# Weight differences and sums of the feed-forward beginnings made by adding transfers, on one Trainium2 core

## The chip, the core and the metric

The kernel runs on one core of a Trainium2 chip. A core has five engines with queues of their own: TensorE (PE, matrix products), VectorE (DVE), ScalarE (ACT), GpSimd (POOL) and SyncE (SP, which here only issues transfers). Transfers run on 16 DMA engines that the queues share. An engine takes its instructions in order; one that waits holds up all behind it on the same engine. The metric is the device time of one execution in microseconds.

## The reference

A two-layer encoder on `x` of 512 tokens by 1024 features, in float32. Only the feed-forward halves are touched by the change:

```python
def swiglu(x, w_gate, w_up, w_down):
    return (jax.nn.silu(x @ w_gate) * (x @ w_up)) @ w_down

for l in range(DEPTH):                                    # DEPTH = 2
    x = x + 0.5 * swiglu(rms_norm(x, ffn1_norm[l]), ffn1_w_gate[l], ffn1_w_up[l], ffn1_w_down[l])
    h = rms_norm(x, mix_norm[l]); p = h @ w_in[l]
    ...                                                   # attention and convolution groups, output projection
    x = x + 0.5 * swiglu(rms_norm(x, ffn2_norm[l]), ffn2_w_gate[l], ffn2_w_up[l], ffn2_w_down[l])
    x = rms_norm(x, post_norm[l])
```

The hidden width is 2816, that is 22 blocks of 128.

## The kernel before

**Precision.** Every float32 operand of PE is split in two numbers of a shorter format: `hi`, the rounded value, and `lo`, the rest. A product is then three matmuls (`mm3`, L145 to L147). The split of a weight of 128x1024 is a cast on ACT (`hi`, tile `wh`, L228) and a subtraction on DVE (`lo`, tile `wl`, L230), both in `split_into`. `wpool` holds four tiles `wh` and four `wl`; a split has to wait until PE has used the tile it takes over.

**Feed-forward.** `ffn_body` is called four times: layer 0 first and second, layer 1 first and second. The work is cut into six units of hidden blocks (`UNITS`), and the weights of a unit come as tiles `fr` of 512 KB, loaded by SP into nine buffers. Unit 0 is `opening()`: four weights, 96 matmuls. At its end the norm is known (`norm()`, a reciprocal root on POOL, L163), and the gate and the transposes (`gated` L356 and L357, `turn` L366) follow. A block goes through DRAM to be turned into the layout of the next product: four small transfers out (`d`, L372) and two back in (`r`, L378), in `moved`; `halved` (L384, L385) splits what came back.

Units 1 to 5 use seven products instead of eight (`product`, named b11, b21, t2, t3, t1, t4, b22; 24 matmuls each). They need sums of weights and of the inputs. The inputs' sums are made by a generator of twelve small steps, which `ops.advance(n)` moves on by n (six in the opening, three times two in unit 1); the steps are `scaled` (L269) and `signed` (L157, L158, in `split_scaled`). The weights' sums are `add`, two halves of 128x1024 each on DVE (L326). In unit 1 the sums a21 and s3 are made already by transfers that add to what is in the buffer (`fetch` with `more`, L318, issued by POOL): eight buffers `fr` and eight `raw` over the four calls. A transfer that adds can only be issued by POOL.

In the output projection eight of the weights take another way to `lo`: ACT writes the negative rounded value (L137), and an adding transfer from DRAM puts the weight on it (L138).

**Between the layers.** The last norm of layer 0 isn't applied to `x` at once. The products of layer 1's first feed-forward use the norm's factor at the gate (`NormPost.__call__`), and `norm.post()` spreads the factor over the partitions (L197 on DVE, L201 on PE, L207 on ACT) and scales the eight blocks of `x` (L973 on DVE) in unit 1. It has to be done before the first down product adds to `x`, which is in unit 2. For the other calls `post` does nothing.

**Order.** The program is written in one stream, and a scheduler of the framework lays down the order of the instructions on each engine; `between(i)` marks where the down products of the unit before are put. In the first call (`lead` is not empty) `x` is still being loaded during the opening.

Of the kernel before, what the change touches and what calls it, by code (L numbers as in the profile page):

```python
# [8 lines left out]
FR = mybir.dt.float32r  # L9
BF = mybir.dt.bfloat16  # L10
I32 = mybir.dt.int32
AF = mybir.ActivationFunctionType
ALU = mybir.AluOpType
AX = mybir.AxisListType

P = 128
# [17 lines left out]
WC = 1024  # L34
HS = S // 2
UNITS = (2, 4, 4, 4, 4, 4)
FIRST = (0, 4, 12, 20, 28, 36)
# [33 lines left out]
def encoder_kernel(ctx: ExitStack, tc: tile.TileContext, xT, consts, vecs, rgain, wgu1, wd1,  # L71
# [6 lines left out]
    wpool = ctx.enter_context(tc.tile_pool(name="w", bufs=4))  # L78
# [6 lines left out]
    def nm(s):  # L85
        uid[0] += 1
        return f"{s}{uid[0]}"
# [4 lines left out]
    def tmp(w=S, dt=FP):  # L92
        return tmps.tile([P, w], dt, tag="t", name=nm("t"))

    def bank():
        return psum.tile([P, S], FP, tag="ps", name=nm("ps"))

    def tiny(tag, w, dt=FP):
        return small.tile([P, w], dt, tag=tag, name=nm(tag))

    V, A, G, T = nc.vector, nc.scalar, nc.gpsimd, nc.tensor
# [23 lines left out]
    def vv(l, name):  # L125
        o, w = VOFF[name]
        return vec[:, l, o:o + w]
# [16 lines left out]
    def mm3(o, lh, ll, rh, rl, first, last, free=False):  # L144
        T.matmul(o, lh, rh, start=first, stop=False, skip_group_check=free)  # L145
        T.matmul(o, lh, rl, start=False, stop=False, skip_group_check=free)  # L146
        T.matmul(o, ll, rh, start=False, stop=last, skip_group_check=free)  # L147
# [68 lines left out]
    def groups(srcs, rhs, ws=None):  # L216
# [5 lines left out]
                group(o, w, rhs, ks, KD)  # L222
        return os

    def split_into(q, src, w=WC):

        hi = wpool.tile([P, WC], FR, tag="wh", name=nm("wh"))
        A.copy(hi[:, :w], src[:, :w])  # L228
        lo = wpool.tile([P, WC], FR, tag="wl", name=nm("wl"))
        V.tensor_tensor(lo[:, :w], src[:, :w], hi[:, :w].bitcast(FP), ALU.subtract)  # L230
        return hi, lo
# [74 lines left out]
    def ffn_body(fpool, l, ops, norm, wgu, wd, done, lead):  # L306
        rt = []

        def wide():
            return fpool.tile([P, 2, S], FP, tag="e", name=nm("e"), bufs=WIDE)  # L310

        def fresh():
            return fpool.tile([P, WC], FP, tag="fr", name=nm("fr"), bufs=FRB)

        def fetch(t, i, more=None):
            nc.sync.dma_start(out=t, in_=wgu[l, i])
            if more is not None:
                G.dma_start(out=t, in_=wgu[l, more], accum_op=ALU.add)  # L318
            return t

        def quarter(u, q):
            return [fetch(fresh(), FIRST[u] + 2 * q + h) for h in range(2)]

        def add(o, a, b):
            for oh, ah, bh in zip(o, a, b):
                V.tensor_tensor(oh, ah, bh, ALU.add)  # L326

        def product(o, ts, n, start, stop):
            w = [split_into("q", t) for t in ts]
            kn = 4 // len(w)  # L330
            N = WC // kn
            for j, k in [(j, k) for j in range(2) for k in range(4)]:
                hi, lo = ops.k[n][k]
                t = slice(j * P, (j + 1) * P)
                c = slice(k % kn * N, (k % kn + 1) * N)
                mm3(o[j][:, :N], hi[:, t], lo[:, t], w[k // kn][0][:, c], w[k // kn][1][:, c],
                    start and k == 0, stop and k == 3, True)

        def copied(o, N):
            w = wide()  # L340
            for j in range(2):
                A.copy(w[:, j, :N], o[j][:, :N])
            return w

        def join(o, a, b, op, N):
            for j in range(2):
                V.tensor_tensor(o[j][:, :N], a[j][:, :N], b[j][:, :N], op)  # L347

        def sides(w):
            return [w[:, j] for j in range(2)]  # L350
# [9 lines left out]
        def block():  # L360
            return fpool.tile([P, 8, P], FP, tag="e", name=nm("e"), bufs=WIDE)

        def turn(to, t, v):

            for j in range(2):
                V.transpose(to[:, :, (2 * t + j) * 32:(2 * t + j + 1) * 32], v[j][:, :HS])  # L366
# [21 lines left out]
        def opening():  # L388
            os = [bank() for _ in range(NT)]
            for i in range(4):  # L390
                w = split_into("q", fetch(fresh(), FIRST[0] + i))
                if lead:
                    lead[i]()
                for k in (2 * i, 2 * i + 1):
                    c = slice(k % 2 * S, (k % 2 + 1) * S)
                    for t in range(NT):
                        hi, lo = ops.k[("b11", "b12", "b21", "b22")[k % 2 * 2 + t // 2]][k // 2]
                        ts_ = slice(t % 2 * P, (t % 2 + 1) * P)
                        mm3(os[t], hi[:, ts_], lo[:, ts_], w[0][:, c], w[1][:, c], k == 0, k == KD - 1)
            ops.advance(6)  # L400
            rt.extend((norm(), tiny("rh", NT)))
            V.tensor_scalar(rt[1], rt[0], 0.5, None, ALU.mult)
            blk = block()
            for t in range(2):
                v = tmp()
                turn(blk, t, gated(t, os[2 * t:2 * t + 2], [v[:, j * HS:(j + 1) * HS] for j in range(2)], S))
            return moved(blk)

        def unit(u, between):
            first = u == 1  # L410
            if first:
                a11, a12 = quarter(u, 0), quarter(u, 1)
                a21 = [fetch(fresh(), FIRST[u] + 4 + h, FIRST[u] + 6 + h) for h in range(2)]
                a22 = quarter(u, 3)
            else:
                a11, a12, a21, a22 = (quarter(u, q) for q in range(4))
            s3 = [wpool.tile([P, WC], FP, tag="raw", name=nm("raw"), bufs=3) for _ in range(2)]
            if first:
                for h in range(2):
                    fetch(s3[h], FIRST[u] + h, FIRST[u] + 4 + h)  # L420
            N = S
            bx = [bank(), bank()]
            product(bx, a11, "b11", True, True)
            a = sides(copied(bx, N))
            between(0)
            by = [bank(), bank()]
            product(by, a12, "b21", True, True)
            if not first:
                add(s3, a11, a21)
                add(a21, a21, a22)  # L430
            add(a11, a11, a21)
            between(1)
            join(a, a, by, ALU.add, N)
            b0 = block()
            turn(b0, 0, gated(0, a, a, N))
            product(bx, a11, "t2", False, True)
            c = sides(copied(bx, N))
            if first:
                ops.advance(2)
            between(2)  # L440
            bz = [bank(), bank()]
            product(bz, s3, "t3", True, True)
            d = sides(copied(bz, N))
            if first:
                ops.advance(2)
            add(a12, a12, a11)
            between(3)
            product(bx, a21, "t1", False, True)
            join(d, d, bx, ALU.subtract, N)
            b1 = block()  # L450
            turn(b1, 1, gated(1, d, d, N))
            if first:
                ops.advance(2)
                norm.post()
            between(4)
            product(bz, a22, "t4", False, True)
            join(c, bz, c, ALU.subtract, N)
            turn(b1, 0, gated(0, c, c, N))
            b1 = moved(b1)
            product(bx, a12, "b22", False, True)  # L460
            s = tmp()
            turn(b0, 1, gated(1, bx, [s[:, j * HS:(j + 1) * HS] for j in range(2)], N))
            return b1 + moved(b0)
# [23 lines left out]
        for u in range(last + 1):  # L487
            f0 = sum(UNITS[:u]) - len(acts)

            def between(i):  # L490
                if i == 0:
                    acts.extend(halved(d) for d in ds)
                elif 1 < u < last:
                    m0 = 2 * i - 2
                    if len(acts) > 4:
                        down(f0 - UNITS[u - 1], acts, (m0, m0 + 1))
                    else:
                        down2(f0 - UNITS[u - 1], acts, m0)
            ds = unit(u, between) if u else opening()
            if 1 < u < last:  # L500
                acts = []
        f0 = sum(UNITS[:-2])
        n0, n = UNITS[-2], UNITS[-2] + UNITS[-1]
# [406 lines left out]
    ops = Operands(vv(0, "g1"))  # L910
# [20 lines left out]
    lead = [fetch((1,)), fetch((2, 3)), fetch((4, 5)), squared((6, 7))]  # L931
    norm = Norm(st)
    for l in range(L):
# [3 lines left out]
        ops, st2, done = lead_in(vv(l, "g2"))  # L937
# [4 lines left out]
        if l + 1 < L:  # L942
# [10 lines left out]
            ops = nops  # L953
# [20 lines left out]
            norm = NormPost(st3)  # L974
        else:
# [4 lines left out]
            for m in range(KD):  # L980
                o = slot()
# [93 lines left out]
```

## Time and profile before

| | |
|---|---|
| time, median of 3 runs | 1817.16 us (1814.3 to 1822.64) |
| the profiled execution | 1818.46 us, its span 1816.7 us |
| mean granted clock of TensorE | 0.993 |
| PE busy | 1761.6 us, 97% of the span |
| DVE busy | 1405.7 us, 77% |
| ACT busy | 949.7 us, 52% |
| POOL busy | 280.1 us, 15% |
| transfers issued by POOL that add | 24 of 512 KB (8 `fr`, 8 `raw`, 8 `wl` of the output projection) |
| `fr` loads by SP, median from issue to landing | 4.0 us |

Times in rows of the profile are us from the start of the span. A row of the timeline reads: start, length, engine, line, operation, output and inputs (buffer numbers left out), count, and in brackets how long the engine stood idle before it and what released it. A row of the waits reads: who waited for whom, us in total, times, longest. A row of the windows reads: the stretch, its length, then for PE, PE's weight loads, DVE, ACT and POOL the busy time and the number of instructions, then the granted clock, the share of the DMA engines, GB/s. In the grouped rows the numbers behind the bar are the busy time in us and the mean of one in ns.

### The profile page before, as it was taken

The page shows a single profiled execution, that of the slowest core. Times are in us where ns is not written, and L with a number is a line of the kernel's source. Part 1 is how long each engine was busy: PE and PEld are TensorE (multiplying, and loading weights), DVE is VectorE, ACT ScalarE, POOL GpSimd, SP SyncE. Part 2 cuts the span into 40 slices and gives each one's busy share as a digit, 9 for nine tenths or more (in the row PEclk, how much of TensorE's full clock was granted, in tenths as well). Part 3 has the DMA queues.
Part 4 walks back from the last instruction along what each step waited for, and adds up shares of the span by engine and source line. Part 5 has one row for each costly group of instructions (what it writes and reads, how often), then busy time and mean ns, then how long its engine had stood idle before and what let it go on. Part 6 is the DMA issues. An engine that isn't in the chain of part 4 may idle for free.

```text
span 1816.7 us, 22175 instructions
## 1 busy us (share of the span) xinstructions
PE 1761.6 (97%) x8160; PEld 1448.8 (80%) x8160; DVE 1405.7 (77%) x1983; ACT 949.7 (52%) x1471; POOL 280.1 (15%) x216
## 2 busy tenths in 40 slices
PE   8899999999899999999998999999999999999997
PEld 6688888888688778888876888888978787788885
DVE  8968887588958968878779678866989679678864
ACT  6444445457954634445544444444778445444442
POOL 4000000048932000000000000000688300000000
PEclk9999999999999999999999999999999999999998
DMA  8344434324124345343924445343250543444241
GB/s 287 122 156 152 149 105 139 117 87 127 37 115 117 125 154 163 113 142 107 286 70 131 136 129 162 105 128 118 74 151 1 161 118 119 159 139 153 91 151 58
DMA packets 119037, 234.09 MB, mean 129 GB/s; under 512 B 10256, under 2 KB 55696, under 8 KB 118928
## 3 DMA queue, kind: packets, MB, share of 16 engines
q1 hardware_dynamic: 115040, 219.72, 36.9%
q0 software_dynamic: 3456, 12.58, 3.9%
q8 instruction: 64, 1.05, 0.2%
q14 instruction: 45, 0.37, 0.1%
q10 hardware_dynamic: 432, 0.38, 0.1%
HBM read 207.47 MB, written 25.17 MB: 128 GB/s over the span
## 4 chain that ended last, share of the span: by engine, by line
PE 65%; issue 19%; DVE 5%; DMA 3%; ACT 3%; POOL 1%; SPq 1%; POOLq 0%; DVEq 0%; ACTq 0%
PE ps L145 20%; PE ps L147 20%; PE ps L146 20%; PE ps L775 2%; PE ps L741 1%; DVE wl L230 1%; DMA fr<-in_wgu 1%; ACT pr L818 1%; DMA r<-d 1%; PE ps L762 1%; DMA d<-e 1%; DVE fr L326 1%; ACT r L747 1%; POOL sck L163 0%; PE ps L201 0%
## 5 line engine op out<-in xcount | busy, mean ns | idle before, releaser
L145 PE MATMUL ps<-wh,r 128*128 128x512 f32 (+2 forms) x1392 | 520.3, 386 | 19.0 <-ACT wh L228 8.5
L147 PE MATMUL ps<-wh,r 128*128 128x512 f32 (+2 forms) x1392 | 530.8, 386 | 7.3 <-DVE r L158 7.1
L146 PE MATMUL ps<-wl,r 128*128 128x512 f32 (+2 forms) x1392 | 532.5, 384 | 0.0
L228 ACT CAST wh<-fr 128x1024 fp32r<-128x1024 f32 x256 | 267.9, 1049 | 239.2 <-PE ps L147 143.4
L147 PE MATMUL ps<-r,wl 128*128 128x512 f32 x1008 | 390.8, 390 | 0.5 <-POOL wl L140 0.5
L146 PE MATMUL ps<-r,wh 128*128 128x512 f32 x1008 | 391.1, 390 | 0.0
L145 PE MATMUL ps<-r,wh 128*128 128x512 f32 x1008 | 385.7, 393 | 3.2 <-ACT r L384 1.8
L230 DVE TENSOR_TENSOR wl<-fr,wh 128x1024 fp32r<-128x1024 f32 x256 | 312.6, 1224 | 76.2 <-ACT wh L228 75.2
L145 PEld LDWEIGHTS ps<-wh,r 128*128 128x128 f32 x1392 | 262.0, 189 | 73.8 <-ACT wh L228 10.3
L147 PEld LDWEIGHTS ps<-wh,r 128*128 128x128 f32 x1392 | 262.4, 189 | 62.5 <-DVE r L158 11.8
L146 PEld LDWEIGHTS ps<-wl,r 128*128 128x128 f32 x1392 | 262.4, 188 | 50.6 <-DVE wl L230 0.5
L134 ACT CAST wh<-raw 128x1024 fp32r<-128x1024 f32 (+2 forms) x150 | 148.8, 996 | 239.3 <-PE ps L146 89.2
L145 PEld LDWEIGHTS ps<-r,wh 128*128 128x128 f32 x1008 | 188.7, 188 | 48.3 <-ACT r L384 4.7
L146 PEld LDWEIGHTS ps<-r,wh 128*128 128x128 f32 x1008 | 189.2, 188 | 42.1 <-DVE r L385 1.8
L147 PEld LDWEIGHTS ps<-r,wl 128*128 128x128 f32 x1008 | 189.2, 188 | 40.8 <-POOL wl L140 1.3
L140 DVE TENSOR_TENSOR wl<-raw,wh 128x1024 fp32r<-128x1024 f32 (+3 forms) x134 | 157.6, 1177 | 76.4 <-ACT wh L134 75.6
L163 POOL TENSOR_TENSOR rtok<-vtok,minus_half 128x4 f32<-128x4 f32 x9 | 12.0, 1329 | 1089.4 <-DVE vtok L189 1089.4
L822 POOL TENSOR_TENSOR y<-y,pr 128x509 f32<-128x509 f32 (+15 forms) x120 | 157.8, 1316 | 49.9 <-ACT pr L818 42.4
L326 DVE TENSOR_TENSOR fr<-fr,fr 128x1024 f32<-128x1024 f32 x112 | 136.7, 1222 | 7.4 <-DMA fr<-in_wgu 7.2
L467 DVE TENSOR_TENSOR x<-ps,x 128x512 f32<-128x512 f32 x128 | 86.5, 686 | 44.1 <-PE ps L147 43.7
L385 DVE TENSOR_TENSOR r<-r,r 128x512 fp32r<-128x512 f32 x88 | 58.4, 682 | 70.7 <-ACT r L384 70.5
L356 ACT ACTIVATE e<-e,rtok 128x256 f32<-128x256 f32 x120 | 59.8, 507 | 71.6 <-DVE e L347 70.7
(164 smaller groups left out, 1724.1 us busy)
## 6 DMA issues: line engine op xcount, KB each, us to landing
fr<-in_wgu SPq DMA_DIRECT2D x176, 512.0 KB, 4.0
raw<-in_wd SPq DMA_DIRECT2D x64, 512.0 KB, 4.5
d<-e SPq DMA_DIRECT2D x176, 128.0 KB, 2.7
r<-d SPq DMA_DIRECT2D x88, 256.0 KB, 4.0
raw<-in_wd SPq DMA_DIRECT2D x32, 384.0 KB, 3.8
raw<-in_wcv SPq DMA_DIRECT2D x16, 512.0 KB, 3.3
raw<-in_wout SPq DMA_DIRECT2D x16, 512.0 KB, 3.7
raw<-in_wgu SPq DMA_DIRECT2D x8, 512.0 KB, 4.7
```

What stands on the lines that cost most here:

```text
L134: A.copy(hi[:, :w], raw[:, :w])
L140: (G if kind in POOLW.split() else V).tensor_tensor(lo[:, :w], raw[:, :w], hi[:, :w].bitcast(FP), ALU.subtract)
L145: T.matmul(o, lh, rh, start=first, stop=False, skip_group_check=free)
L146: T.matmul(o, lh, rl, start=False, stop=False, skip_group_check=free)
L147: T.matmul(o, ll, rh, start=False, stop=last, skip_group_check=free)
L228: A.copy(hi[:, :w], src[:, :w])
L230: V.tensor_tensor(lo[:, :w], src[:, :w], hi[:, :w].bitcast(FP), ALU.subtract)
L326: V.tensor_tensor(oh, ah, bh, ALU.add)
L356: A.activation(out[j][:, :h], src[j][:, :h], AF.Silu, scale=r)
L385: V.tensor_tensor(d, d.bitcast(FP), hi.bitcast(FP), ALU.subtract)
L467: V.tensor_tensor(xm, pd.rearrange("p (a t j) -> p t a j", a=4, t=NT), xm, ALU.add)
L822: order["conv"] = G.tensor_tensor(acc[:, s:], acc[:, s:], pr[:, s:], ALU.add).ins
```

## The change

It does four things. (1) A new `split_adding` takes the way of the output projection for seven weights of a call: the four of the opening (not in the first call, where `lead` is set) and in unit 1 the two of b11 and the first of b21. (2) In unit 1 the two sums a11 + a21 and a12 + a11 become adding transfers from buffer to buffer (`gather`), four per call. (3) The operand steps of `ops.advance` in unit 1 stand one product sooner. (4) `norm.post()` moves from unit 1, behind t1, to the beginning of unit 2.

```diff
+    def split_adding(src, again):
+
+        hi = wpool.tile([P, WC], FR, tag="wh", name=nm("wh"))
+        A.copy(hi, src)
+        lo = wpool.tile([P, WC], FR, tag="wl", name=nm("wl"))
+        A.activation(lo, src, AF.Copy, scale=-1.0)
+        G.dma_start(out=lo, in_=again, accum_op=ALU.add)
+        return hi, lo
...
-        def product(o, ts, n, start, stop):
-            w = [split_into("q", t) for t in ts]
+        def product(o, ts, n, start, stop, adding=()):
+            w = [split_adding(t, wgu[l, i]) for t, i in zip(ts, adding)]
+            w += [split_into("q", t) for t in ts[len(w):]]
...
         def opening():
             os = [bank() for _ in range(NT)]
             for i in range(4):
-                w = split_into("q", fetch(fresh(), FIRST[0] + i))
+                w = fetch(fresh(), FIRST[0] + i)
+                w = split_into("q", w) if lead else split_adding(w, wgu[l, FIRST[0] + i])
...
+            def gather(o, b):
+                if not first:
+                    return add(o, o, b)
+                for oh, bh in zip(o, b):
+                    G.dma_start(out=oh, in_=bh, accum_op=ALU.add)
+
...
-            product(bx, a11, "b11", True, True)
+            product(bx, a11, "b11", True, True, (FIRST[u], FIRST[u] + 1) if first else ())
             a = sides(copied(bx, N))
             between(0)
             by = [bank(), bank()]
-            product(by, a12, "b21", True, True)
+            if first:
+                ops.advance(2)
+            product(by, a12, "b21", True, True, (FIRST[u] + 2,) if first else ())
...
-            add(a11, a11, a21)
+            gather(a11, a21)
...
-            product(bx, a11, "t2", False, True)
-            c = sides(copied(bx, N))
             if first:
                 ops.advance(2)
+            product(bx, a11, "t2", False, True)
+            if first:
+                ops.advance(2)
+            c = sides(copied(bx, N))
             between(2)
...
-            if first:
-                ops.advance(2)
-            add(a12, a12, a11)
+            gather(a12, a11)
...
-            if first:
-                ops.advance(2)
-                norm.post()
             between(4)
...
             def between(i):
+                if u == 2 and i == 0:
+                    norm.post()
```

Lines move down with it: the cast, the negative rounding and the adding transfer of `split_adding` are L228, L230 and L231, the subtraction of `split_into` is L239, `fetch`'s are L325 (SP) and L327 (POOL), `add` is L335, `gather`'s transfer L437, `gated` L367 on DVE, `turn` L376, `moved` L382 and L388, the scaling L992.

POOL's queue in the first call; `fr65` and `fr66` are the halves of a21, `raw69` and `raw70` those of s3, `fr61` and `fr62` those of a11, `fr63` and `fr64` those of a12. Before:

```order
L178 TENSOR_TENSOR acc33_248<-acc33_248,t39_265 128x512
L318 DMA fr65_364<-in_wgu1 128x1024
L318 DMA fr66_367<-in_wgu1 128x1024
L318 DMA raw69_374<-in_wgu1 128x1024
L318 DMA raw70_375<-in_wgu1 128x1024
L163 TENSOR_TENSOR rtok53_328<-vtok51_321,minus_half_88 128x4
```

After:

```order
L178 TENSOR_TENSOR acc33_248<-acc33_248,t39_265 128x512
L231 DMA wl74_384<-in_wgu1 128x1024
L231 DMA wl76_389<-in_wgu1 128x1024
L327 DMA fr65_364<-in_wgu1 128x1024
L327 DMA fr66_367<-in_wgu1 128x1024
L231 DMA wl87_437<-in_wgu1 128x1024
L327 DMA raw69_374<-in_wgu1 128x1024
L327 DMA raw70_375<-in_wgu1 128x1024
L163 TENSOR_TENSOR rtok53_328<-vtok51_321,minus_half_88 128x4
L437 DMA fr61_356<-fr65_364 128x1024
L437 DMA fr62_358<-fr66_367 128x1024
L437 DMA fr63_360<-fr61_356 128x1024
```

Two differences stand ahead of the four sums that were there, one stands among them, and four transfers between buffers follow (the fourth, to `fr64`, is left out here); `wl87` is b21's.

SP's queue in the second call, around the blocks of the opening that go out (`d1036`) and come back (`r1037`, `r1038`); the `fr` are weights. Before:

```order
L316 DMA fr1113_5508<-in_wgu2 128x1024
L372 DMA d1036_5139<-e1033_5124 32x8x128 x4
L316 DMA fr1114_5510<-in_wgu2 128x1024
L316 DMA fr1115_5512<-in_wgu2 128x1024
L378 DMA r1037_5144<-d1036_5139 128x512
L378 DMA r1038_5146<-d1036_5139 128x512
```

After:

```order
L325 DMA fr1113_5518<-in_wgu2 128x1024
L382 DMA d1036_5146<-e1033_5131 32x8x128 x4
L325 DMA fr1114_5520<-in_wgu2 128x1024
L388 DMA r1037_5151<-d1036_5146 128x512
L388 DMA r1038_5153<-d1036_5146 128x512
L325 DMA fr1115_5522<-in_wgu2 128x1024
```

One weight load has moved from ahead of the two loads of r to behind them.

DVE in the third call (layer 1, first feed-forward), at the scaling of `x` by `R`. Before, the first of four such pairs:

```order
L158 SCALAR_TENSOR_TENSOR r1567_8008<-r1513_7794,r1566_8007 128x512
L269 SCALAR_TENSOR_TENSOR r1575_8048<-x_78,gc1002_4958,r1509_7782 128x256 x2
L973 SCALAR_TENSOR_TENSOR x_78<-x_78,vec_80,R1594_8123 128x512 x2
L230 TENSOR_TENSOR wl1596_8135<-fr1539_7870,wh1595_8133 128x1024
L326 TENSOR_TENSOR raw1618_8246<-fr1610_8230,fr1614_8238 128x1024
```

After:

```order
L367 SCALAR_TENSOR_TENSOR e1579_8053<-e1579_8053,rh1526_7844 128x256
L992 SCALAR_TENSOR_TENSOR x_78<-x_78,vec_80,R1626_8292 128x512 x8
L335 TENSOR_TENSOR fr1610_8239<-fr1610_8239,fr1608_8235 128x1024
L376 STREAM_TRANSPOSE e1591_8129<-e1579_8053 128x8x32 x2
L357 TENSOR_TENSOR e1623_8285<-e1623_8285,ps1631_8314 128x512
L357 TENSOR_TENSOR e1623_8285<-e1623_8285,ps1632_8315 128x512
L140 TENSOR_TENSOR wl1643_8384<-raw1641_8380,wh1642_8382 128x768
L239 TENSOR_TENSOR wl1647_8417<-fr1607_8233,wh1646_8415 128x1024
```

The eight scalings have become one block, behind unit 1's last gate and ahead of the split of the weights of unit 2 (`wl1647`); before, they lay in pairs among unit 1's splits and sums.

## The prediction

> **What bounds the kernel now.** I read the page's engine line first, then the table of waits of TensorE, then windows of 25 us to find where these waits lie, and last the timelines of those places. The sum below is made against the profiled execution, whose span is 1816.7 us and whose run took 1818.46; that is 1.3 us above the median of the three runs shown, 1817.16, and I take the same difference off either. They spread over 8.3 us, so about 0.5%, 9 us, is what a measurement can tell from no change.
>
> ```profile
> PE 1761.6 (97%) x8160; PEld 1448.8 (80%) x8160; DVE 1405.7 (77%) x1983; ACT 949.7 (52%) x1471; POOL 280.1 (15%) x216
> ...
> fr<-in_wgu POOLq DMA_DIRECT2D x8, 512.0 KB, 6.7
> ```
>
> TensorE (PE) has 55 us of idle time in all, and 97% of the span is its own work, which the change leaves as it is. So no version of it can give back more than a part of 55 us. Which part, the waits say:
>
> ```profile
> PE ps L147 <- DVE r L158: 7.1, 6, 2.0
> PE ps L145 <- ACT r L157: 5.9, 3, 2.8
> PE ps L145 <- DVE e L347: 4.5, 4, 2.0
> ```
>
> These three, 17.5 us, are the operands of the products and the joined halves of unit 1: work of VectorE (DVE), or of ScalarE (ACT) behind a late transfer. The windows put them into the four feed-forward beginnings; of each row the first pair is PE, the third DVE.
>
> ```profile
> 50.00:75.00 25.00, 20.28 (x77) 15.36 (x78) 22.01 (x34) 14.47 (x22) 0.00 (x0) 0.93 0.43 146
> 575.00:600.00 25.00, 25.00 (x115) 20.81 (x115) 17.27 (x25) 10.64 (x15) 1.04 (x1) 1.00 0.26 83
> 600.00:625.00 25.00, 22.47 (x94) 17.07 (x94) 22.55 (x34) 15.88 (x22) 0.00 (x0) 1.00 0.42 143
> 950.00:975.00 25.00, 20.51 (x87) 15.99 (x86) 23.64 (x35) 11.84 (x17) 0.00 (x0) 0.99 0.35 120
> ```
>
> In the three rows where PE falls to 20 to 22 us, DVE is busy 22.0 to 23.6 of 25: there it is the bound. In the row before B's (575 to 600) PE has no idle time and DVE 7.7 us of it. I call the four places A (layer 0, first feed-forward, 0 to 100 us), B (layer 0, second, 530 to 660), C (layer 1, first, 870 to 1010) and D (layer 1, second, like B).
>
> **What is removed and added.** Prices per instruction:
>
> ```profile
> L230 DVE TENSOR_TENSOR wl<-fr,wh 128x1024 fp32r<-128x1024 f32 x256 | 312.6, 1224 | 76.2 <-ACT wh L228 75.2
> L326 DVE TENSOR_TENSOR fr<-fr,fr 128x1024 f32<-128x1024 f32 x112 | 136.7, 1222 | 7.4 <-DMA fr<-in_wgu 7.2
> L137 ACT ACTIVATE wl<-raw 128x1024 fp32r<-128x1024 f32 x8 | 8.4, 1054 | 0.0
> ```
>
> Seven differences in B, C and D and three in A are 24 subtractions, and two sums of two halves in four places are 16 additions: 40 x 1.22 = 49 us leave DVE. ACT gets 24 x 1.05 = 25 us, and it has 48% of the span free. GpSimd (POOL) and the 16 DMA engines get 40 adding transfers of 512 KB, 24 of them from HBM and 16 between buffers. Most of the 49 us lies where DVE waits anyway: the openings' twelve differences in B, C and D belong to stretches like 575 to 600. That part is worth nothing, and its cover is PE's own 96 matmuls of the opening. What counts is the end of each chain.
>
> **A: three differences and two sums.** The GB/s row is the load of the DMA engines in 40 slices of 23 to 50 us, 0.675 us each; then what POOL and SP issued, and on PE the first matmuls of b21 and of t2 and the stalls.
>
> ```profile
> GB/s 437 425 401 437 419 407 340 170 212 225 206 200 212 194 219 212 225 200 212 194 225 103 30 6 0 0 0 0 0 161 209 268 206 182 425 146 197 367 419 394
> ```
> ```profile
> 23.83 1.95 POOL L318 DMA_DIRECT2D fr<-in_wgu  x2
> 25.30 2.25 POOL L318 DMA_DIRECT2D raw<-in_wgu  x2
> ```
> ```profile
> 41.84 1.86 SPq L372 DMA_DIRECT2D d<-e  x4
> ```
> ```profile
> 37.93 0.39 PE L145 MATMUL ps<-wh,r 128*128 128x512 f32 x1
> ...
> 43.37 0.61 PE L145 MATMUL ps<-wh,r 128*128 128x512 f32 x2
> ...
> 51.80 0.50 PE L145 MATMUL ps<-wh,r 128*128 128x512 f32 x1 [2.83 <-ACT r L157]
> ...
> 61.24 0.50 PE L147 MATMUL ps<-wh,r 128*128 128x512 f32 x1 [0.98 <-DVE r L158]
> ...
> 64.91 0.50 PE L147 MATMUL ps<-wh,r 128*128 128x512 f32 x1 [0.65 <-DVE r L158]
> ...
> 69.20 0.50 PE L145 MATMUL ps<-wh,r 128*128 128x512 f32 x1 [1.28 <-DVE e L347]
> ```
>
> The plain loads end at about 28 us at over 400 GB/s; then, until 37.2, the four adding transfers run alone at about 210. 512 KB at 210 GB/s is 2.5 us each, and a fourth ends about 37 to 39. POOL can't issue earlier, since it sums squares until 23.83. In the new order eleven adding transfers stand in this queue. Counting 2.5 us each from a first landing at about 32, the two differences of b11 land at 32 and 34.5, when they are needed. The two halves of a21 land at 37 and 39.5, and b21's difference, fifth, at 42. PE wants its low half at 38.2 (b21 begins at 37.93): a stall of about 3.7. Two sums for t3 follow (44.5, 47), then the halves of the new a11 (49.5, 52). t2 needs the first of them plus a cast of 1.05: 50.5, where 43.37 + 3.7 = 47.1 would have done: 3.4 more. Its second weight costs some 0.7. So t3 begins near 50.5 + 0.7 + 5.4 = 56.6, or 57.5 with the operands behind it, against 51.80. The transposed blocks' small transfers, 512 KB out and 512 KB in, start at 41.84 and now share the engines with this queue: at 400 GB/s up to another 2.5.
>
> What is given back: the 2.83 before t3 is inside this sum already. DVE has seven operations fewer (8.5 us) by then, and the three later stalls, 0.98 + 0.65 + 1.28 = 2.9, go. Net: +5.2 - 2.9 = 2.3, with the shared engines about **+3 us, slower**. Lower end: if the queue were fast enough, all four stalls would go, -5.7; upper end: +5.7 with 2.5 of sharing and nothing given back, +8.
>
> The Trainium skill ("DMA: Bandwidth & Descriptors", Anatomy of one DMA) fits such a transfer from GpSimd with about 2.0 us plus its bytes at 436 GB/s, an estimate of 3.2 us here and 1.2 us between two in a row. By that rule the a11 halves would land before 42 us, in time. The trace disagrees: 210 GB/s at full engines, and 6.7 us median to landing. The fit speaks of HBM to SBUF without an addition, so I go by the row.
>
> **B and D: four differences of the opening, three of unit 1, two sums.** DVE at the gate, the chain behind it, and PE's stalls in B and D:
>
> ```profile
> 587.84 1.22 DVE L326 TENSOR_TENSOR fr<-fr,fr 128x1024 f32<-128x1024 f32 x1
> ```
> ```profile
> 596.27 4.90 DMA r<-d
> ...
> 602.35 0.64 ACT r L157
> ```
> ```profile
> 603.03 0.50 PE L145 MATMUL ps<-wh,r 128*128 128x512 f32 x1 [0.34 <-ACT r L157]
> ...
> 614.39 0.50 PE L147 MATMUL ps<-wh,r 128*128 128x512 f32 x1 [1.40 <-DVE r L158]
> ...
> 618.06 0.50 PE L145 MATMUL ps<-wh,r 128*128 128x512 f32 x1 [0.65 <-DVE e L347]
> ```
> ```profile
> 1511.48 0.50 PE L147 MATMUL ps<-wh,r 128*128 128x512 f32 x1 [1.57 <-DVE r L158]
> ...
> 1515.14 0.50 PE L145 MATMUL ps<-wh,r 128*128 128x512 f32 x1 [0.61 <-DVE e L347]
> ```
>
> Here the weights of the opening wait in their buffers 20 us ahead, so each adding transfer has a whole product of 5.4 us against 2.5: hidden. The last sums land near 593, for a weight wanted after 600. The addition at 587.84 stood between the gate's scale and its first multiplication; without it the chain to the transposes and to SP's small transfers starts nearly its 1.22 us sooner. Of two weight loads on SP ahead of the loads of r, one now stands behind them; r's 4.90 us should shrink by about 1.2, a plain 512 KB at 400 GB/s. So r lands about 2 us sooner and DVE runs 2 us ahead of its old times until it is the bound again. PE's quoted stalls in B are 2.4 and in D 2.2; with a rest of 0.5 each I take **-1.8 for B and -1.7 for D**. Bounds: -2.4 and -2.2; and 0, if the small transfers meet the last sums on the engines.
>
> **C: the same, and post norm's scaling one unit later.** DVE at the gate, PE's stalls, and DVE where the scaling now goes:
>
> ```profile
> 927.75 1.22 DVE L326 TENSOR_TENSOR fr<-fr,fr 128x1024 f32<-128x1024 f32 x1
> ...
> 930.64 0.68 DVE L197 TENSOR_TENSOR t<-cst,rtok 128x512 f32<-128x512 f32 x1
> ```
> ```profile
> 946.24 0.50 PE L145 MATMUL ps<-wh,r 128*128 128x512 f32 x1 [2.75 <-ACT r L157]
> ...
> 955.96 0.50 PE L147 MATMUL ps<-wh,r 128*128 128x512 f32 x1 [0.54 <-DVE r L158]
> ...
> 960.95 0.50 PE L147 MATMUL ps<-wh,r 128*128 128x512 f32 x1 [1.98 <-DVE r L158]
> ...
> 965.94 0.50 PE L145 MATMUL ps<-wh,r 128*128 128x512 f32 x1 [1.97 <-DVE e L347]
> ```
> ```profile
> L973 DVE SCALAR_TENSOR_TENSOR x<-x,vec,R x8: 745/749/756, 950.2 to 971.1; 128x512 f32<-128x512 f32 x8
> ```
> ```profile
> 990.41 2.36 DVE L230 TENSOR_TENSOR wl<-fr,wh 128x1024 fp32r<-128x1024 f32 x2
> ```
>
> Two operations leave the gate's chain, 1.22 and 0.68 us; a new adding transfer stands on POOL between the two reciprocal roots and takes back about 0.7. So r is some 1.1 us sooner, and the 2.75 becomes 1.6. The eight scalings, 8 x 0.75 = 6 us of DVE, leave 950 to 972, so the other three stalls (4.5) go there. But all eight come back in one block, ahead of the difference at 990.41, which PE waits for in the very stretch where DVE has no free time (23.64 of 25 us in the window). What PE gains by 972 it then waits for at 985 to 990. DVE's work up to that difference is the same sum, so C gains what the gate gains and some idle time of DVE: **-2.5**. Bounds: -7.2 (all four stalls), and 0. The sums sooner (the advanced operand steps) and the order on ACT cost no instruction; they lie in the same DVE sum, and I price them at nothing; if that cover fails, one operation of 128x512 (0.68 us, the row at 930.64) per product is late.
>
> **Sum.** +3 - 1.8 - 1.7 - 2.5 = -3 us: 1813.7 for the span, 1815.5 for such a run, 1814 by the median.
>
> **Rivals.**
> One, slower: the queue on POOL is not served at 2.5 us. The longest of the sixteen here took 12.9 us to land:
>
> ```profile
> DMA to landing us min/median/max: 5.4/7.0/12.9
> ```
>
> If the seven that stand ahead of A's first sum followed each other at 5.4 us, the lowest of these landings, instead of 2.5, t2 would begin 7 x 2.9 = 20 us later: +17 in all, 1834. It decides, +9, from a spacing of 4.2 us on. For it speaks that transfers between buffers were never run here; against it the even 210 GB/s.
>
> Two, the relief is whole: A's transfers come in time, and all quoted stalls go: 5.7 + 2.4 + 2.2 + 7.2 = 17.5 us, 1800. Against it speaks the GB/s row in A.
>
> Three, the scaling finds room in unit 2: C gives 7.2 instead of 2.5, 1809.
>
> Four, A alone is fast, because adding runs nearer to a plain load's 400 GB/s: A gives -3 instead of +3, 1808. The skill's fit would make this one.
>
> **Chances.** Forecast 0.50 (its own range 1808 to 1820), rival one 0.12, two 0.15, three 0.13, four 0.10. Faster by over 0.5% (below 1808): two whole, half of four, parts of three and of the forecast, 0.28. Slower (above 1826): most of one and a tail of the forecast, 0.12. Within: 0.60. The range 1803 to 1824 leaves out most of one and of two.
>
> **What would show it.** In A: PE stalls of 3 to 4 us at b21 and at t2, released by ACT casts or an adding transfer, and fewer stalls on r L158 later. In B and D: no adding transfer releases PE; r lands near 599; stalls of 0.5 where 2.3 were. In C: a stall of about 1.6 before t3, almost none until 972, then one of 4 to 5 near 985 released by DVE's wl. DVE's total falls by 49 us, ACT's rises by 25. I am wrong if the queue in A lands at 1.2 or at over 4 us spacing, or if no stall follows the block of eight.

## The result, and the profile after

The changed kernel takes 1839.58 us (median of 4, 1837.03 to 1844.54), the kernel before beside it 1816.99. The ratio is 1.0123 with a 95% interval of 1.0105 to 1.0142: about 22 us slower, outside the range that was given, and on the other side of "no change". The page of the changed kernel, the engines, two kinds of POOL's transfers and the queue that carries them:

```profile
span 1837.4 us, 22263 instructions
...
PE 1772.3 (96%) x8160; PEld 1457.5 (79%) x8160; DVE 1361.2 (74%) x1943; ACT 970.2 (53%) x1495; POOL 314.9 (17%) x256
...
q0 software_dynamic: 9216, 33.56, 9.5%
...
wl<-in_wgu POOLq DMA_DIRECT2D x24, 512.0 KB, 11.3
...
fr<-fr POOLq DMA_DIRECT2D x16, 512.0 KB, 8.5
```

DVE lost 44 us of work and ACT gained 20 (49 and 25 were costed). But the adding transfers now take 11.3 and 8.5 us to land, where 6.7 was the median before. PE is idle for 65 us instead of 55, and is 10.7 us longer "busy" with the same 8160 matmuls: after its long stalls it runs some us at a lower clock (its mean granted clock is 0.986, before 0.993). So longer waits are only half of the 20.7 us between the two profiled executions. The waits of PE:

```profile
PE ps L145 <- ACT wh L237: 11.8, 2, 7.7
PE ps L146 <- DMA wl<-in_wgu: 7.7, 7, 2.3
PE ps L147 <- DVE r L158: 6.6, 6, 3.4
PE ps L145 <- ACT r L157: 5.4, 3, 2.6
PE ps L147 <- DVE wl L140: 5.2, 1, 5.2
...
PE ps L145 <- DVE e L357: 1.3, 2, 0.6
```

The first row was 8.5 before, and its 7.7 us at the start of the kernel are in both; the other 4.1 are a stall in A. The second and the fifth row are new; of the three rows that the prediction began with, 17.5 us before, 13.3 are still there.

**Where the time went.** Both kernels have the same 8160 matmuls, so the delay can be read place by place: the start of PE's n-th matmul in one kernel's timeline minus the start of the same matmul in the profiled execution of before. A column gives this delay in us at a place; only its growth along a row counts, since separate runs differ by 1 to 3 us in places that no edit touches.

```
matmul n                      420   2500  2760   3060  3960  4200   4340  4500   6600  6850   7100
place                       end A  ahead  end of  end  ahead end of  972  end C  ahead end of  end
                                    of B  opening  B   of C  opening  us         of D  opening  D
changed kernel                9.9   10.0  12.4   11.8  12.0  14.3   10.2  16.5   16.4  19.0   20.1
e1 first call plain          -1.7   -3.1   0.1    2.0   2.1   4.9    0.9   8.2    7.9  10.4   11.0
e2 openings plain             9.5    9.6   9.6   12.2  11.7  11.7    8.1  13.9   13.8  13.8   14.7
e3 scaling back               7.0    6.7   9.1    9.8  10.0  12.8   13.0  11.6   12.2  14.8   15.5
e4 first call, sums plain     0.5   -0.4   2.1    4.9   5.3   6.3    1.8   7.5    9.0  11.5   11.8
e5 steps only                -2.4   -2.5  -2.5   -2.6  -3.3  -3.3   -3.8  -3.7   -3.4  -3.4   -3.7
e6 unit 1's adding only      -0.4   -1.7  -1.7   -1.7  -2.4  -2.4   -2.2  -3.6   -2.1  -2.1   -1.1
e9 half of the openings       9.5    8.2   8.2   10.3   9.6   9.7    5.2  12.6   12.0  12.0   11.8
e10 late scaling alone       -1.3   -2.6  -2.6   -2.6  -3.0  -3.0   -9.7  -3.4   -3.6  -3.6   -4.3
e13 adding, no load wait      6.2    6.0   6.1    2.8   2.3   2.3   -0.7   2.8    2.7   2.7    0.3
e14 steps, no load wait       3.8    3.0   3.0   -0.3  -0.6  -0.6   -2.0   0.4    0.4   0.4   -2.7
e15 scaling on ACT and POOL  -2.7   -3.6  -3.6   -3.4  -3.3  -3.3   -7.9  -1.9   -2.7  -2.7   -2.8
```

In the changed kernel A costs 9.9 us, the three openings 2.4, 2.3 and 2.6, the rest of B gives 0.6 back, C's unit 1 gives 4.0 and then loses 6.3, and D loses another 1.1: together about 20 of the 20.7 us. Undone one at a time, A (e1), the openings (e2) and the scaling (e3) take 9.1, 5.4 and 4.6 off the 20.1 us at the end of D; by the ratios of the medians it is some 13, 12 and 6 of 22, each with some 5 us to either side.

**A.** PE's stalls there, then the transfers of 23 to 60 us (GB/s in 40 slices) and the median landing of the four small ones that carry the opening's block out:

```profile
41.49 0.50 PE L146 MATMUL ps<-wl,r 128*128 128x512 f32 x1 [2.29 <-DMA wl<-in_wgu]
50.85 1.22 PE L145 MATMUL ps<-wh,r 128*128 128x512 f32 x2 [4.08 <-ACT wh L237]
60.99 0.79 PE L145 MATMUL ps<-wh,r 128*128 128x512 f32 x1 [2.64 <-ACT r L157]
```
```profile
GB/s 425 421 425 416 341 199 213 217 208 208 208 213 213 213 213 213 213 217 199 213 195 220 230 195 221 223 197 219 234 189 285 247 219 159 51 337 213 221 255 416
...
d<-e SPq DMA_DIRECT2D x4, 128.0 KB, 13.5
r<-d SPq DMA_DIRECT2D x2, 256.0 KB, 4.6
```

From 27 to about 50 us all engines run at some 210 GB/s: adding transfers, one behind the other. b21 waits for its difference (2.29), t2 for the cast of its sum (4.08), as forecast, and t3 for r (2.64): the four small transfers took 13.5 us instead of 2 to 2.3, which was not forecast. The halves of the new a11 landed at 49.7 and 52.5, where the prediction had 49.5 and 52, so POOL's queue moved as it said. After t2's stall the delay grows by another 1.9 us, from 7.5 to 9.4 between 50.85 and 55.22, without a wait: matmuls start 0.43 to 0.67 us apart there, and 0.23 where the clock is full.

**The openings.** PE in B's opening (C and D show the same two rows, 0.52 and 1.09, 0.80 and 1.20) and POOL ahead of it:

```profile
574.48 0.50 PE L146 MATMUL ps<-wl,r 128*128 128x512 f32 x1 [0.63 <-DMA wl<-in_wgu]
581.42 0.50 PE L146 MATMUL ps<-wl,r 128*128 128x512 f32 x1 [1.20 <-DMA wl<-in_wgu]
```
```profile
562.93 1.21 POOL L231 DMA_DIRECT2D wl<-in_wgu  x1
566.82 0.86 POOL L327 DMA_DIRECT2D fr<-in_wgu  x1 [2.67 <-DMA fr<-in_wgu]
568.02 0.88 POOL L231 DMA_DIRECT2D wl<-in_wgu  x1 [0.34 <-ACT wl L230]
```

The first difference was issued at 562.93 and landed at 574.4, the second at 568.02 and landed at 581.4, behind three and four sums. One of these sums made POOL wait 2.67 us for a load, with the second difference behind it.

**C.** The block of eight on DVE (its last seven) and PE's wait:

```profile
996.52 4.72 DVE L992 SCALAR_TENSOR_TENSOR x<-x,vec,R 128x512 f32<-128x512 f32 x7
...
1004.15 0.94 DVE L140 TENSOR_TENSOR wl<-raw,wh 128x768 fp32r<-128x768 f32 x1
```
```profile
1005.15 0.79 PE L147 MATMUL ps<-r,wl 128*128 128x512 f32 x1 [5.16 <-DVE wl L140]
```

### The profile page after: what moved, and what is told of

Read it like the earlier page. It is cut to its first block, busy times and chain, and to the rows that moved or that the text cites. A ratio compares the mean times of both kernels' runs of the same rounds, so it can differ in the third digit from the quotient of the medians.

```text
span 1837.4 us, 22263 instructions
## 1 busy us (share of the span) xinstructions
PE 1772.3 (96%) x8160; PEld 1457.5 (79%) x8160; DVE 1361.2 (74%) x1943; ACT 970.2 (53%) x1495; POOL 314.9 (17%) x256
## 5 line engine op out<-in xcount | busy, mean ns | idle before, releaser
L237 ACT CAST wh<-fr 128x1024 fp32r<-128x1024 f32 x232 | 242.8, 1049 | 211.3 <-PE ps L147 105.1
L239 DVE TENSOR_TENSOR wl<-fr,wh 128x1024 fp32r<-128x1024 f32 x232 | 283.7, 1225 | 67.4 <-ACT wh L237 66.1
L146 PEld LDWEIGHTS ps<-wl,r 128*128 128x128 f32 x1392 | 264.5, 190 | 63.3 <-DMA wl<-in_wgu 10.7
L140 DVE TENSOR_TENSOR wl<-raw,wh 128x1024 fp32r<-128x1024 f32 (+3 forms) x134 | 157.2, 1174 | 75.4 <-ACT wh L134 74.6
L841 POOL TENSOR_TENSOR y<-y,pr 128x511 f32<-128x511 f32 (+14 forms) x120 | 157.9, 1316 | 51.8 <-ACT pr L837 44.3
L335 DVE TENSOR_TENSOR fr<-fr,fr 128x1024 f32<-128x1024 f32 x96 | 116.7, 1215 | 7.6 <-DMA fr<-in_wgu 7.6
## 6 DMA issues: line engine op xcount, KB each, us to landing
wl<-in_wgu POOLq DMA_DIRECT2D x24, 512.0 KB, 11.3
```

What stands on the lines that cost most here:

```text
L140: (G if kind in POOLW.split() else V).tensor_tensor(lo[:, :w], raw[:, :w], hi[:, :w].bitcast(FP), ALU.subtract)
L841: order["conv"] = G.tensor_tensor(acc[:, s:], acc[:, s:], pr[:, s:], ALU.add).ins
```

## The experiments

Two theories for the loss: **Q**, the adding transfers (their rate, their queue, and what shares the DMA engines with them), and **O**, the new order of the operand steps and of DVE and ACT around them. **S** and **L** below are on the scaling and on why DVE's relief was worth nothing.

**e1, e4: A without adding transfers, and without the sums alone.**

The first edit is in both, the second in e1 alone, with a like one at b21.

```diff
-                if not first:
+                if not first or lead:
                     return add(o, o, b)
...
-            product(bx, a11, "b11", True, True, (FIRST[u], FIRST[u] + 1) if first else ())
+            product(bx, a11, "b11", True, True, (FIRST[u], FIRST[u] + 1) if first and not lead else ())
```

> The first call (A) as before: differences and sums of its unit 1 on DVE; the other three calls as changed. Theory Q (adding transfers: the queue on POOL lands one every 2.5 to 3.5 us and small transfers beside it wait with it): PE's delay against before, 9.9 us at 150 us in the changed kernel, goes to within 0.7; the 2.4 us steps in the other openings stay; about 1830. Theory O (the order: operand steps one product sooner and what the scheduler made of it): several of the 9.9 us stay, 1835 or more.

Measured: 1829.78 beside 1820.79, ratio 1.0052 (1.0031 to 1.0073); the delay at A's end is -1.7. The 9.9 us are gone, and O falls for A: the steps sooner cost nothing there (six runs have them in A without a new adding transfer, e1, e5, e6, e7, e10 and e15, and stand between -2.7 and -0.1).

> In the first call only the two sums go back to DVE; the three differences stay adding transfers. Theory Q: POOL's queue ends near 47 us instead of 59, the small transfers out, 13 us to landing in the changed kernel, take until about 47 still, t2's stall of 4.2 us goes, that at b21 (2.45) stays: delay at 150 us about 5. If the sums alone were guilty: under 1. If the differences alone: 9.

Measured: ratio 1.0063 (1.0046 to 1.0081), 0.5 at A's end. So the two sums cost 9.4 of A's 9.9, and the three differences about 2 beside e1's -1.7. The delay at 150 us was not 5 but 0.5. PE makes good almost 4 us between 53 and 67, and loses 3 at 97 to 101, where it waits for unit 1's block and a down weight.

**e8: the same bytes on the same queue, without adding** (in A only; the values of the sums are left out).

```diff
-                G.dma_start(out=t, in_=wgu[l, more], accum_op=ALU.add)
+                G.dma_start(out=t, in_=wgu[l, more], **({} if lead else dict(accum_op=ALU.add)))
...
-                    G.dma_start(out=oh, in_=bh, accum_op=ALU.add)
+                    G.dma_start(out=oh, in_=bh, **({} if lead else dict(accum_op=ALU.add)))
```

> The changed kernel, but in the first call the eight sum transfers on POOL's queue copy and do not add (the values of those sums are left out); same queue, same bytes, same order. If adding is what takes 2.5 us per 512 KB: the eight land 1.2 to 1.4 us apart, POOL's queue ends near 45, the small transfers out take 4 to 6 us instead of 13, and the delay at 150 us falls from 9.9 to 2 or 3. If POOL's queue itself is that slow, whatever it carries: spacing 2.5, and 9 to 10 us.

Measured, in two executions: ratio 1.0064 (1.0042 to 1.0085), delay 0.4 at A's end. The DMA view of 23 to 60 us in e8:

```profile
GB/s 421 416 425 421 376 204 208 213 226 204 332 412 390 213 217 239 394 394 421 421 417 358 311 239 394 354 233 359 350 334 412 221 31 257 310 0 133 412 22 142
...
d<-e SPq DMA_DIRECT2D x4, 128.0 KB, 6.3
```

The stretches near 210 are the differences, which still add; the copies run at 390 to 420 and land 1.2 to 1.4 us apart. It is the adding that halves the rate, not POOL's queue. And the small transfers follow: 13.5 us in the changed kernel, 8.6 in e4, 6.3 here, and in e1, where the queue is empty when they start:

```profile
d<-e SPq DMA_DIRECT2D x4, 128.0 KB, 2.2
```

In each of the first three the last of the four lands within 1.2 us after the last transfer that POOL had issued when they were issued (it landed at 52.5, 47.1 and 44.6 us). They don't stand still until then. The queues of POOL (`q0`) and SP (`q1`) in the changed kernel from 42 to 50 us, with packets, MB and share of the engines' time:

```profile
q0 software_dynamic: 416, 1.51, 94.4%
q1 hardware_dynamic: 416, 0.20, 12.6%
```

Packet for packet they move alike. But a packet of the small transfers carries about 0.5 KB and one of POOL's 3.6, so the small ones get 25 GB/s beside POOL's 189. From 51 to 52 us, when POOL's queue has thinned out, they move 0.23 MB, more than in those 8 us.

The Trainium skill ("DMA: Bandwidth & Descriptors", SWDGE vs HWDGE vs iDMA) says that the two kinds of queue feed different queues inside each DMA engine, which the engine serves in turn. The trace agrees: 416 packets of each. What this costs a queue of short packets is in the 13.5, 8.6, 6.3 and 2.2 us.

**e2, e9: the openings without adding transfers, and with them for the last two weights only.**

```diff
-                w = split_into("q", w) if lead else split_adding(w, wgu[l, FIRST[0] + i])
+                w = split_into("q", w)                                                                       # e2
+                w = split_into("q", w) if lead or i < 2 else split_adding(w, wgu[l, FIRST[0] + i])           # e9
```

> The openings' four differences on DVE again in the second to fourth call, all else as changed. Theory Q: the delays of 2.4, 2.3 and 2.6 us inside the three openings, at low halves that PE waits for, go, nothing comes in their place, since DVE was idle there: about 1832. Theory O: the openings' steps go, but the units behind them lose as much, 1838.

Measured: ratio 1.0057 (1.0040 to 1.0074), 1830.99. The steps inside all three openings are 0.0. In B, though, the rest of the call then loses 2.6, where the changed kernel gave back 0.6. That is what O said, in one place of three, but it isn't the order: the rest of B is the same in e1, e3, e4, e6 and e9 too, and reads 1.9, 0.7, 2.8, 0.0 and 2.1. What spreads it from -0.6 to 2.8 isn't shown.

> The changed kernel, but of the four weights of each opening (second to fourth call) the first two are split on DVE again and only the last two by adding transfers. Theory Q says that the first two were late because of their place in POOL's queue, behind three sums: the last two now have two fewer ahead and 5 us more, so the steps of 2.4, 2.3 and 2.6 us in the openings fall below 0.4 each: 1831, as with all four on DVE. If an adding transfer is late by itself (the extra pass on ACT, the transfer's own length), half of each step stays: 1835.

Measured: ratio 1.0068 (1.0055 to 1.0082); the steps are 0.0, 0.1 and 0.0. So an adding transfer is not late by itself. That the first two were late by their place behind the sums is read from POOL's rows above: they took 11.5 and 13.4 us to land, and one that stood alone in e2 took 5.4. No run put them ahead of the sums.

**e3, e10, e15: the scaling.** e3 puts it back to unit 1; e10 is the kernel before with the steps sooner and the scaling late; e15 the same with the scaling off DVE.

```diff
-                        V.scalar_tensor_tensor(x[:, m, :], x[:, m, :], gp[:, m:m + 1], Rp, ALU.mult, ALU.mult)
+                        A.activation(x[:, m, :], x[:, m, :], AF.Copy, scale=gp[:, m:m + 1])      # e15
+                        G.tensor_tensor(x[:, m, :], x[:, m, :], Rp, ALU.mult)
```

> Only post norm's scaling goes back to unit 1. Theory S (the block of eight is what PE waits for at 1005 us): the 5.8 us lost there go, the 4.0 us gained between 950 and 972 are lost again, and PE's one wait for DVE's low half of a down weight, 5.2 us, is gone: 1837 to 1838. Rival: that wait has another cause (the load of the down weight) and stays: 1843.

Measured: 1834.80, ratio 1.0089 (1.0063 to 1.0114). Between 931 and 1011 us the delay falls by 1.2, where it grew by 2.2 in the changed kernel, and the wait for L140's low half is gone: the block was its cause, and by the delays the move cost 3.4 us, not 2. The time lies below both forecasts.

> The kernel before with the steps sooner and with post norm's scaling on DVE at the beginning of unit 2; no new adding transfer. Theory S: in the third call PE gains some 4.5 us between 950 and 972 and loses 5 to 6 at the block of eight: beside the kernel with the steps alone (delay -3.9 at the end of the profile) it ends near -2.5, the time is the same within 2 us. If the block was only bad because the queue on POOL had made everything late: -8, faster by 4.

Measured: ratio 1.0010 (1.0000 to 1.0020). PE gains 6.7 in C by 972 and gives back 6.3 at the block. The trade is even without the queue.

> The kernel with the steps sooner and post norm's scaling off DVE, at the beginning of unit 2: the gains on ACT, the factor on POOL, eight of each. Theory S: PE keeps the 7 us that it is ahead in the third call at 973 us in the run with the late scaling on DVE, and the 5.8 us at the block are not lost: 1811. Rival: POOL's eight multiplications hold up DVE operations beside them, as in the run with POOL's sums (one of 0.9 us took 5.1), and nothing is gained: 1817 or more.

Measured: ratio 1.0000 (0.9990 to 1.0010). PE gains 4.7 and loses 6.0. POOL's eight multiplications, and a DVE operation beside them that takes 1.22 us elsewhere:

```profile
974.83 14.97 POOL L975 TENSOR_TENSOR x<-x,R 128x512 f32<-128x512 f32 x8 [47.77 <-ACT R L207]
```
```profile
975.05 2.31 DVE L326 TENSOR_TENSOR fr<-fr,fr 128x1024 f32<-128x1024 f32 x1
```

The rival held: work that was put on POOL came back as longer DVE operations.

**e5, e6, e7: what is left when the guilty parts are undone.** e5 is before with the operand steps as in the change; e6 the change without adding in A and in the openings and with the scaling back; e7 the same with the sums on DVE.

```diff
+            if first:                               # e5, ahead of b21; likewise around t2
+                ops.advance(2)
             product(by, a12, "b21", True, True)
```

> The kernel before with the operand steps one product sooner and nothing else. Theory Q: they are harmless; the first call gains the 1.7 us that PE is ahead there in the run with the first call plain, the other calls stay within 1: 1815 to 1818 beside a before of 1817 to 1821. Theory O: the second and fourth call lose 2 to 3 us in their unit 1, as in the changed kernel: 1822 or more.

Measured: ratio 1.0004 (0.9991 to 1.0017). Harmless; no loss in B (-0.1) or D (-0.3). O falls there too.

> What is left of the change: in the second to fourth call, unit 1's three differences and four sum halves by adding transfers, and the steps sooner; first call and openings plain, scaling back. By the delays of the runs before: -1.7 in the first call, +2.6 in the second, -1 in the third, +1 in the fourth: within 3 us of before. If DVE's relief were worth something once the queue is short: 6 us or more faster.

Measured: ratio 1.0001 (0.9991 to 1.0012). With the three places undone the loss is gone. Seven adding transfers a call, for none of which PE waits, gain nothing.

> As the run before this one, with the sums on DVE too: only three differences per call (second to fourth) are adding transfers. Theory Q: a short queue with 5 us per product costs nothing: -1.7 of the first call and no loss elsewhere, 2 to 4 us faster than before. If the second call's +2.6 belongs to the differences or the steps rather than to the sums, it stays.

Measured: ratio 1.0009 (1.0000 to 1.0019). The 2 to 4 us did not come.

**e11 to e14: why the relief of DVE gains nothing.** Unit 2's first sum stands in DVE's order inside unit 1. DVE there in e6, and PE's two stalls behind it:

```profile
606.77 1.22 DVE L239 TENSOR_TENSOR wl<-fr,wh 128x1024 fp32r<-128x1024 f32 x1
609.81 1.23 DVE L335 TENSOR_TENSOR raw<-fr,fr 128x1024 f32<-128x1024 f32 x1 [1.82 <-DMA fr<-in_wgu]
```
```profile
612.83 0.50 PE L147 MATMUL ps<-wh,r 128*128 128x512 f32 x1 [2.73 <-DVE r L158]
...
616.49 0.50 PE L145 MATMUL ps<-wh,r 128*128 128x512 f32 x1 [0.65 <-DVE e L357]
```

DVE comes sooner and then waits for a weight load, which waits for a buffer that an earlier split on DVE sets free. SP's waits in e6 from 600 to 615 us:

```profile
SPq L325 <- DVE wl L239: 8.7, 4, 3.8
```

e11 (on e6) and e12 (on e5) put that sum on POOL; e13 (on e6) and e14 (on e5) let it add a11 to itself.

```diff
-                add(s3, a11, a21)
+                add(s3, a11, a21, G if u == 2 else V)        # e11, e12
+                add(s3, a11, a11 if u == 2 else a21)         # e13, e14
```

> The kernel with unit 1's three differences and the sums by adding transfers in the second to fourth call, and besides unit 2's first sum (two halves) on POOL instead of DVE. Theory L: in unit 1 of the second and fourth call the gain was lost because DVE, in order, stood 1.8 to 2.1 us at that sum, which waits for a weight load that waits for a buffer; with the sum elsewhere the stalls of 2.9 and 0.8 us before t1 and t4 go: 2 to 3 us in each of these calls against the same kernel without this, 1812. If DVE's own work is the bound: 1 us each.

> The kernel before with the steps sooner and unit 2's first sum on POOL; no new adding transfer. Theory L: here too DVE no longer stands at the load, 1 to 2 us per call in the second, third and fourth: 1813. If it is as fast as the run with the adding transfers, these are worth nothing even where they are hidden. If POOL's additions (2.4 to 2.9 us for 128x1024 in the output projection) slow DVE beside them, no gain.

Measured: 1.0062 (1.0049 to 1.0075) and 1.0064 (1.0051 to 1.0078), both slower. POOL and DVE in e12:

```profile
615.01 5.62 POOL L326 TENSOR_TENSOR raw<-fr,fr 128x1024 f32<-128x1024 f32 x2 [23.60 <-DMA fr<-in_wgu]
```
```profile
615.81 5.10 DVE L269 SCALAR_TENSOR_TENSOR r<-x,vec,r 128x256 f32<-128x256 f32 x2
```

Two operations of 0.87 us together took 5.10, until POOL was done. These two runs say nothing on L.

> The kernel with unit 1's differences and sums by adding transfers in the second to fourth call (openings and first call plain, scaling back), and in unit 2 the first sum adds a11 to itself instead of a21, so that it waits for no late load (the values of that product are left out). Theory L: DVE's idle 1.8 us at that sum goes; with the sum itself ahead of the tight stretch, PE's stalls of 2.9 and 0.8 us before t1 and t4 fall below 1: 2 to 3 us per call, 1811 to 1814. If PE waits as long as before, the loads were not what kept the relief back.

> The same in the kernel with the steps sooner and no new adding transfer: unit 2's first sum adds a11 to itself (values left out). Theory L: here DVE is itself busy, so the gain is smaller than in the run with the adding transfers by the 1 to 2 us per call that DVE is relieved of: 1813 to 1816. If both gain alike, the adding transfers relieve nothing that counts.

Measured: 0.9991 (0.9981 to 1.0000) and 0.9988 (0.9979 to 0.9997). In A both stand 4 to 6 us behind: in e13 DVE takes the sum ahead of r there and hands the opening's block out 2 us later, and t3's wait for r is 5.88 us where it is 2.93 in e6. In B and D it helps. In B this row

```profile
618.10 0.50 PE L147 MATMUL ps<-wh,r 128*128 128x512 f32 x1 [0.18 <-DVE r L158]
```

is all that is left of PE's two stalls in e13. The delay falls by 3.3 in B and 2.4 in D in e13, and by 3.3 and 3.1 in e14. So L holds in part: that sum, with its wait, cost about 3 us per call in either kernel. But with it out of the way the kernel with the adding transfers gains no more than the one without: the relief itself is worth nothing that these runs can show.

No kernel here beats the one before by more than its interval with the whole computation.

## Why the prediction was wrong

By its own steps:

- **A, "+3 us": the sign and the place were right, the size wrong; 9.9.** The stalls at b21 and t2 were forecast as 3.7 and 3.4 and came as 2.3 and 4.1. One step that failed is the sharing of the engines, "at 400 GB/s up to another 2.5", of which the sum took 0.7. The small transfers took 13.5 us; r came late, and t3 began at 60.99 against 57.5 plus 2.5 at most. The 400 GB/s were the rate of plain loads; beside POOL's adding transfers the small ones got 25. The other is a cost that the sum doesn't have: the 1.9 us of slower matmuls behind t2's stall. The second term, "2.9 given back", did come (3.2 us between 63 and 76), but as much was lost again at 106 to 114 us, where PE waits for unit 1's block and a down weight. The forecast's 5.2 ahead of it isn't worked out: its own times for t3 give 4.8 or 5.7.
- **B and D, "each adding transfer has a whole product of 5.4 us against 2.5: hidden": wrong.** I counted a transfer against its own product, and not its place in the queue. The first weights' differences were issued at 562.93 and 568.02, behind the sums of unit 1, which had nothing to hurry for. It cost 2.4, 2.3 and 2.6 us, in C's opening too. In e9, where the last two of the four have two transfers fewer ahead and the first two are split on DVE, nothing is late.
- **B and D, "-1.8" and "-1.7": r sooner, as forecast (its two halves by 2.5 and 1.4 us against PE's matmuls in B), and the 0.34 before t3 is gone in B, but the stall moved.** B gave back 0.6 after its opening, and D lost 1.1. The step that failed is "DVE runs 2 us ahead until it is the bound again": I had read DVE as the bound, and did not see the load that the row of DVE's first sum waits for; e13 and e14 show the 3 us that this sum holds with its wait.
- **C, "-2.5": the mechanism was right, both sizes off.** PE gained 4.0 by 972 (forecast 4.5, and 1.1 at the gate, which did not come: t3 still waited 2.62), and lost 5.16 in one wait at the block, over 6 with the low clock after it, where I had 4 to 5. By e3 against the changed kernel the move costs 3.4.
- **The whole sum: only waits had a price.** 10.7 of the 20.7 us are longer busy time of the same matmuls. The sum put the slower clock behind a long stall at nothing, without a reason, though the row 50 to 75 of before, which it shows, reads 0.93 beside a stall of 2.83.
- **None of the four rivals was right.** Rival one named the queue on POOL, but by a spacing of 4.2 us or more. The spacing was 1.8 to 2.8 in A, near the forecast's 2.5, and 2.5 to 3.9 in B's opening; the loss came through what stood beside and behind the queue. That it came out slower, as rival one had it, is luck.

The choice of the row over the fit was right. Adding transfers landed 2.5 us apart and more. The Trainium skill's fit for a transfer from GpSimd ("DMA: Bandwidth & Descriptors", Anatomy of one DMA) gives the estimate of 1.2 us between two, and e8's copies, 1.2 to 1.4, come close to it.

## What to carry to other kernels

Cost an adding transfer by the rows of adding transfers: here twice the engine time of a copy, and while several stood in the queue, small transfers of short packets beside them were late until it thinned out. Place in a queue is a cost of its own: what is wanted first must be issued first, and urgent work behind unhurried sums waits for all of them. A long stall of PE has a second price, the slower matmuls behind it. Before an engine is relieved, look at what its in-order stream waits for in the tight stretch; if it is a load or a buffer, taking work off the engine can only make the wait longer, as in e6 (1.82 us, where e5 has 0.78).

## What was not expected of the hardware

- An adding transfer of 512 KB, one behind the other in A, took 2.5 to 2.8 us of all engines, from HBM and between buffers alike; copies on the same queue took 1.2 to 1.4. Four transfers of 128 KB on another queue took 13.5 us beside them instead of 2.2.
- POOL's operations on tiles held up DVE: an addition of 1.22 us took 2.31 beside POOL's multiplications, and two of 0.87 together 5.10. The Trainium skill ("SBUF — State Buffer", SBUF: two separate sides) describes a port pair that the two engines share as a lock held for a whole instruction; the rows of e12 and e15 agree.
- After its long stalls PE's granted clock was lower; in the changed kernel these windows hold stalls of 4.08 and 2.64 us, and of 5.16:

```profile
50.00:75.00 25.00, 21.17 (x76) 16.06 (x76) 19.68 (x25) 15.78 (x22) 1.72 (x2) 0.86 0.75 225
1000.00:1025.00 25.00, 19.85 (x78) 16.25 (x79) 16.30 (x24) 8.86 (x14) 0.00 (x0) 0.86 0.56 174
```

It is 0.86, where the window of before at 50 us had 0.93 and most have 1.00. The stall of 2.29 us at 41.49 left its window at 1.00; where the limit lies isn't shown. Behind the 5.16 us the delay grew by another 2 us: such a stall costs more than its length.
